# Mixer of a hybrid streaming encoder: readers of freshly loaded decay rows issued behind the eviction of the product traced last

## The chip, the cores and the metric

The kernel runs on one core of one Trainium2 chip. The metric is the device time of one execution in microseconds; the kernel before took 1926.99 us, the median of three runs (1923.51 to 1927.07).

## The reference

One layer of an encoder is computed for 512 prompt frames and 64 sample frames, 576 columns together, with 1024 channels: a SwiGLU block, a mixer, a second SwiGLU block, and a last RMSNorm. The mixer is one wide input projection that feeds three branches, whose outputs are projected, gated, added and projected once more. Two of the branches contain exponentials of cumulated decays, and they are what the change touches. Cut to that:

```python
# branch A, 16 heads in 4 groups, per chunk
cum  = jnp.cumsum(dtc * a, axis=1)
lmat = jnp.exp(jnp.where(causal, cum[:, :, None] - cum[:, None, :], -jnp.inf))
y = einsum((C B^T) * lmat * dt, x) + jnp.exp(cum) * einsum(C, h)
wd = jnp.exp(last[:, None] - cum) * dtc
h = jnp.exp(last) * h + einsum(wd, B, x)
# branch C, 4 heads, per chunk
s = einsum(q, k) * jnp.exp(logd - mt)
num = einsum(s, v) + jnp.exp(inter - mt) * einsum(q, c)
c = decay * c + einsum(jnp.exp(wlog - mnew), k, v)
```

Branch B is a banded softmax attention. All of it is in float32.

## The kernel before, in words

**Products.** Each weight product is made of three matmuls per block of 128 channels, since a float32 weight is split into a high and a low part (`split`, L333 to 335: ScalarE casts `ph`, VectorE subtracts for `pl`). In the mixer, weights come in pairs of columns and a pair takes seven products by Strassen's scheme (`pairs`, L608, over `stream`, L575). One product is 12 matmuls on TensorE (L704) into a PSUM bank `acc`. The pairs have three banks in turn, so a bank has to be evicted within a product or two, or TensorE stands still. Evictions are ScalarE copies (`uv` at L621, direct ones at L628 into `g`, `P` or `R`) and VectorE sums (L630). GpSimd adds weight blocks (L560) and issues accumulating loads of them (L548); SyncE issues the other loads.

**Jobs.** The branches are generators (`attn`, `ml` for branch C, `ssd` for branch A). They are traced a step at a time between the products (`tick`), so that their small matmuls fill in between. The order of the units is `a0 a1 m0 s0 a2 a3 s1 m1 s2 m2 s3 m3`; a unit `s` has two halves, each of two heads.

**Decay rows.** `gates` writes the cumulated decays of all heads to DRAM (`scr_rows`). `decays` (L188, on ScalarE's queue) loads two rows, spread over 128 partitions, into two slots of `R1`, named `R` in the profile; three such pairs of slots go round, and a load is issued one half unit ahead of its use. A half unit of `ssd` reads the rows with VectorE (`wd`, L1333 and L1334; the difference to all columns, L1349) and ScalarE (`el`, L1336 and L1337); then `wd` is exponentiated (L1338), the difference goes through Relu and Exp (L1352, L1358), is multiplied by `cb` on VectorE (L1360) and feeds the matmuls L1393. A second copy of the rows is loaded into the single buffer `ec` (L1356, two DMAs on ScalarE's queue), exponentiated (L1384) and used at L1403. A unit of `ml` reads its rows into the tile `D`, named `P` (L1162 on VectorE), exponentiates it (L1164, L1165), multiplies it by the causal mask on GpSimd (L1167, L1168) and by the scores on VectorE (L1173, L1176); `wc` (L1180) reads the rows on ScalarE.

**What sets the order.** Every engine carries out its instructions in the order in which they stand in its own queue. That order is made when the kernel is built, by a scheduler that plays the program through on a timeline of its own and takes what it holds ready, the tracing order deciding among equals; `high_priority(offset=EVAC)` puts evictions ahead. An edge (`issue_after`) makes the instructions traced within it stand behind a given instruction on that instruction's engine.

Of the kernel before, what the change touches and what calls it, by code (L numbers as in the profile page):

```python
# [28 lines left out]
AF = mybir.ActivationFunctionType  # L29
ALU = mybir.AluOpType  # L30
# [5 lines left out]
CH = [(0, 128), (128, 128), (256, 128), (384, 128), (512, 64)]  # L36
# [49 lines left out]
class Hybrid:  # L86
    def __init__(self, ctx, tc, I, O):
        self.tc, self.nc, self.I, self.O = tc, tc.nc, I, O
        self.op = None
        self.stay = {}  # L90
        self.plan = []
        self.splan = []
        self.ahead = {}
        self.steps = None
        self.b_i, self.b_n, self.fetched = 0, 0, deque()
        self.behind = 0
        self.jobs, self.gap, self.side = deque(), 0, iter(())
        nc = self.nc
        self.const = ctx.enter_context(tc.tile_pool(name="const", bufs=1))
        self.dram = ctx.enter_context(tc.tile_pool(name="scr", bufs=1, space=bass.MemoryType.DRAM))  # L100
        c = self.const
        self.R1 = c.tile([128, 8, T], F32, name="R1")
        self.rs = c.tile([128, T], F32, name="rs")
        self.small = ctx.enter_context(tc.tile_pool(name="small", bufs=8, reuse_waits="tile"))

        self.wt = ctx.enter_context(tc.tile_pool(name="wt", bufs=1, reuse_waits="tile"))
        self.xs = self.dram.tile([128, 8, T], F32, name="xs")

        self.ys = [self.dram.tile([128, T], F32, name=f"ys{i}") for i in range(16)]
        self.gs = [self.dram.tile([128, T], F32, name=f"gs{i}") for i in range(24)]  # L110
        self.scr = self.dram.tile([24, T], F32, name="scr_rows")
# [496 lines left out]
    def pairs(self, seq):  # L608

        nc = self.nc
        order = ((0, self.T_X1), (0, self.T_A11), (1, self.T_A22), (0, self.T_X4), (0, self.T_X3), (1, self.T_X2),
                 (0, self.T_A21))
        H = (slice(0, FH), slice(FH, T))

        def tmp(ps, scale):
            o = self.gp.tile([128, FH], F32, name="uv", tag="uv", bufs=4)
            with self.tc.high_priority(offset=EVAC):  # L620
                nc.scalar.activation(o, ps, AF.Copy, scale=scale)  # L621
            return o

        def emit(ps, scale, other=None, op=None):
            def go(dst, a=0, b=FH, func=None):
                with self.tc.high_priority(offset=EVAC):
                    if other is None:
                        nc.scalar.activation(dst, ps[:, a:b], func or AF.Copy, scale=scale)  # L628
                        return
                    nc.vector.scalar_tensor_tensor(dst, ps[:, a:b], scale, other[:, a:b], op0=ALU.mult, op1=op)  # L630
                if func:
                    nc.scalar.activation(dst, dst, func)
            return go

        def pair(tiles, done):
            ((name, c1), s1, put1), ((_, c2), s2, put2) = tiles
            o = {}

            def on(t, ps):
                if t == self.T_X1:  # L640
                    o["v"] = tmp(ps, s1)
                elif t == self.T_X4:
                    o["m6"] = tmp(ps, s2)
                elif t == self.T_A11:
                    put1(1, H[1], emit(ps, s1, o["v"], ALU.add))
                elif t == self.T_X3:
                    o["u"] = tmp(ps, s2)
                elif t == self.T_A21:
                    put2(1, H[1], emit(ps, s2, o["u"], ALU.subtract))
                elif t == self.T_A22:  # L650
                    put2(0, H[0], emit(ps, -s2, o["m6"], ALU.add))
                else:
                    put1(0, H[0], emit(ps, s1))
                    if done:
                        done()
            return (name, 0, c1, c2), self.T, on

        self.stream([pair(*p) for p in seq], order, lambda n: {self.T_X1: n % 2, self.T_X4: 2, self.T_A11: 2})

    def tick(self):
        next(self.side, None)
# [479 lines left out]
    def ml(self, h, t):  # L1144
        nc = self.nc
        q, k, v, o = t["q"], t["k"], t["v"], t["o"]
        i = self.b()
        nmB, eiB = self.R1[:, i, :], self.R1[:, i + 1, :]
# [6 lines left out]
        self.tok_major(v, v1)  # L1155
        yield 1
        qt = self.t("t")
        nc.gpsimd.tensor_tensor(qt, q, eiB, op=ALU.mult)

        D = self.P()  # L1160
        for c, (a, n) in enumerate(CH):
            nc.vector.tensor_scalar(D[:n, a:a + n], nmB[:n, a:a + n], self.TM[:n, c, 64 + h:65 + h], 0.0,  # L1162
                                    op0=ALU.add, op1=ALU.min)
        nc.scalar.activation(D[:, :512], D[:, :512], AF.Exp)  # L1164
        nc.scalar.activation(D[:64, 512:], D[:64, 512:], AF.Exp)  # L1165
        dv = D[:, :512].rearrange("p (c t) -> p c t", t=128)
# [2 lines left out]
        s = self.ps("s")  # L1169
# [6 lines left out]
        self.empties(nc.vector.tensor_tensor(D[:64, 512:], s2[:64, :64], D[:64, 512:], op=ALU.mult))  # L1176

        wc = self.unit([128, 8], "wc", 2)
        for c, (a, n) in enumerate(CH):
            nc.scalar.activation(wc[:n, c:c + 1], self.TM[:n, c, 64 + h:65 + h], AF.Exp, bias=nmB[:n, a + n - 1:a + n])  # L1180
        yield 2
        nums = [self.ps("v"), self.ps("x")]
        where = [(0, 0), (0, 129), (0, 258), (1, 0), (1, 129)]
# [1 line left out]
        for c, (a, n) in enumerate(CH):  # L1185
# [7 lines left out]
            if c == 0:  # L1193
                i = nc.vector.tensor_copy(C2[:, :129], pc[:, :129])
# [4 lines left out]
            b, o0 = where[c]  # L1199
# [12 lines left out]
        for c, (a, n) in enumerate(CH):  # L1212
            b, o0 = where[c]
# [68 lines left out]
    def ssd(self, g, t):  # L1282
# [26 lines left out]
        for j in range(2):  # L1309
# [18 lines left out]
            wd = self.unit([128, 5, 2], "wd", 2)  # L1328
            el = self.unit([128, 5, 2], "el", 2)
            nc.gpsimd.memset(wd[:, 4, :], 0.0)  # L1330
            for r in range(2):
                last = cum[r][:, 127:512:128]
                nc.vector.tensor_tensor(wd[:, 0:4, r], last, self.TM[:, 0:4, 32 + d0 + r], op=ALU.subtract)  # L1333
                nc.vector.tensor_tensor(wd[:64, 4:5, r], cum[r][:64, 575:576], self.TM[:64, 4:5, 32 + d0 + r],  # L1334
                                        op=ALU.subtract)
                nc.scalar.activation(el[:, 0:4, r], last, AF.Exp)  # L1336
                nc.scalar.activation(el[:, 4:5, r], cum[r][:, 575:576], AF.Exp)  # L1337
            nc.scalar.activation(wd, wd, AF.Exp)  # L1338
            for n, cs in ((128, slice(0, 4)), (64, slice(4, 5))):
                m = cs.stop - cs.start  # L1340
                nc.vector.tensor_tensor(h4(xw[:n, cs, :]), h4(xd[:n, cs, :]),
# [3 lines left out]
            for n, cs, ts in ((128, slice(0, 4), slice(0, 512)), (64, slice(4, 5), slice(512, T))):  # L1345
                m, w = cs.stop - cs.start, ts.stop - ts.start
                e = E[:n, :, ts].rearrange("p r (c t) -> p r c t", c=m)
                tm = self.TM[:n, cs, 32 + d0:34 + d0].rearrange("p c r -> p r c")
                nc.vector.tensor_tensor(e, e, tm.unsqueeze(3).broadcast_to([n, 2, m, w // m]), op=ALU.subtract)  # L1349
                parts.append(E[:n, :, ts])  # L1350
            for e in parts:
                nc.scalar.activation(e, e, AF.Relu, scale=-1.0)  # L1352
# [11 lines left out]
            for c, (a, n) in enumerate(CH):  # L1364
# [16 lines left out]
                    nc.sync.dma_start(self.O["s"][c - 3, :, d0 * 64:d0 * 64 + 128], new)  # L1381
                if c % 2:
                    yield 1
            nc.scalar.activation(ec, ec, AF.Exp)  # L1384
            D = self.cst[:, C_D + 2 * g + j:C_D + 2 * g + j + 1]
            py, pi = self.ps("v"), self.ps("x")
            for c, (a, n) in enumerate(CH):
# [364 lines left out]
```

## Time and profile before

| what | value |
|---|---|
| median of three runs | 1926.99 us (1923.51 to 1927.07) |
| the profiled execution | 1925.69 us, span 1924.0 us |
| TensorE busy in the span | 1865.2 us (97%) |
| VectorE, ScalarE, GpSimd busy | 1532.9, 1058.1, 654.1 us |
| first SwiGLU block, mixer, second SwiGLU block | about 0 to 570, 570 to 1355, 1355 to 1924 us |
| the stretch with pairs and jobs | 625 to 1195 us, TensorE busy 532.9 of 570.0 us |

A row of a timeline gives the start from the beginning of the span, the duration, the engine, the line, the operation and its tiles; idle time of the engine just before it stands in brackets with what ended it. The letter q after an engine marks its queue, that is, an issue of a DMA. In the view of waits a row gives who waited, for whom, the total in microseconds, how often, and the longest.

### The profile page before, as it was taken

Reading aid. Unit: us, or ns where it says so; the run is one execution under the profiler, and the core shown is the slowest. Engines: PE = TensorE matmul, PEld = TensorE weight load, DVE = VectorE, ACT = ScalarE, POOL = GpSimd, SP = SyncE. Lnnn points to the kernel's source line nnn. Section 1 sums busy time; section 2 is a strip of 40 time slices with the busy share of each in tenths; the row PEclk is TensorE's granted clock in tenths of the full one; section 3 lists DMA queues with packets and bytes.
Section 4 is the critical chain, followed back from the end, with each engine's and each line's share of the span. In section 5 each row is a group of like instructions: output and inputs, shape, how many; then the busy total and the mean of one; then the engine's idle time right before and its main releaser. Section 6 shows DMA issues by size and latency. Waiting matters only on the chain. (4 is left out here: it accounts for less than half of the span.)

```text
span 1924.0 us, 37528 instructions
## 1 busy us (share of the span) xinstructions
PE 1865.2 (97%) x13901; PEld 1815.5 (94%) x13901; DVE 1532.9 (80%) x2763; ACT 1058.1 (55%) x2342; POOL 654.1 (34%) x613
## 2 busy tenths in 40 slices
PE   9899999999999989999989989999999999999998
PEld 9899999999999879888989889999999999999998
DVE  7998998998768868678687766745898888898865
ACT  6554554554544776676665556324565455554544
POOL 3443333333302324323334333440334343333311
PEclk9999999999999999999999999999999999999999
DMA  7467666666742546755656655642546666666631
GB/s 222 104 158 177 154 164 159 156 176 164 184 135 89 146 130 161 214 147 144 176 141 183 171 143 173 208 175 82 128 111 159 170 159 166 164 156 169 153 99 56
DMA packets 129439, 294.69 MB, mean 153 GB/s; under 512 B 14288, under 2 KB 26192, under 8 KB 129256
## 3 DMA queue, kind: packets, MB, share of 16 engines
q1 hardware_dynamic: 99368, 203.42, 32.9%
q0 software_dynamic: 20272, 74.20, 21.1%
q10 hardware_dynamic: 9616, 14.69, 2.5%
q8 instruction: 109, 1.79, 0.4%
q14 instruction: 74, 0.61, 0.1%
HBM read 272.87 MB, written 19.38 MB: 152 GB/s over the span
## 5 line engine op out<-in xcount | busy, mean ns | idle before, releaser
L704 PE MATMUL acc<-TH,ph 128*128 128x288 f32 x3220 | 970.3, 302 | 34.2 <-ACT uv L621 16.4
L704 PE MATMUL acc<-TL,ph 128*128 128x288 f32 x3220 | 956.2, 297 | 0.8 <-DVE TL L335 0.7
L704 PE MATMUL acc<-TH,pl 128*128 128x288 f32 x3220 | 953.3, 296 | 0.3 <-DVE pl L335 0.3
L704 PEld LDWEIGHTS acc<-TH,ph 128*128 128x128 f32 x3220 | 607.8, 189 | 53.7 <-ACT uv L621 18.6
L704 PEld LDWEIGHTS acc<-TH,pl 128*128 128x128 f32 x3220 | 609.9, 190 | 2.9 <-issue 2.1
L704 PEld LDWEIGHTS acc<-TL,ph 128*128 128x128 f32 x3220 | 609.1, 189 | 3.0 <-DVE TL L335 2.0
L335 DVE TENSOR_TENSOR pl<-wr,ph 128x512 fp32r<-128x512 f32 x471 | 430.3, 919 | 70.3 <-ACT ph L334 59.0
L334 ACT CAST ph<-wr 128x512 fp32r<-128x512 f32 x471 | 287.2, 618 | 263.8 <-PE acc L704 142.5
L334 ACT CAST ph<-wx 128x512 fp32r<-128x512 f32 x390 | 237.1, 619 | 213.5 <-POOL wx L560 101.4
L335 DVE TENSOR_TENSOR pl<-wx,ph 128x512 fp32r<-128x512 f32 x390 | 312.3, 804 | 46.3 <-ACT ph L334 39.8
L560 POOL TENSOR_TENSOR wx<-wx,wr 128x512 f32<-128x512 f32 x160 | 246.5, 1540 | 178.9 <-DVE pl L335 143.6
L548 POOL DMA_DIRECT2D wx<-in_sblk x115 | 101.6, 917 | 522.3 <-DVE pl L335 204.4
L279 PE MATMUL acc<-YH,ph 128*128 128x256 f32 (+1 forms) x768 | 227.1, 298 | 3.0 <-ACT g L628 2.2
L279 PE MATMUL acc<-YL,ph 128*128 128x256 f32 (+1 forms) x768 | 227.1, 297 | 0.6 <-DVE YL L392 0.6
L279 PE MATMUL acc<-YH,pl 128*128 128x256 f32 (+1 forms) x768 | 226.7, 296 | 0.0
L279 PEld LDWEIGHTS acc<-YH,ph 128*128 128x128 f32 x768 | 145.0, 189 | 4.1 <-ACT g L628 2.3
L279 PEld LDWEIGHTS acc<-YL,ph 128*128 128x128 f32 x768 | 145.3, 189 | 1.1 <-DVE YL L392 1.0
L279 PEld LDWEIGHTS acc<-YH,pl 128*128 128x128 f32 x768 | 145.2, 189 | 0.0
L560 POOL TENSOR_TENSOR wy<-wx,wr 128x512 f32<-128x512 f32 x35 | 49.9, 1425 | 134.0 <-DVE pl L335 112.6
L743 DVE SCALAR_TENSOR_TENSOR R<-acc,R 128x288 f32<-128x288 f32 x168 | 75.7, 451 | 20.1 <-PE acc L704 19.8
L334 ACT CAST TH<-g 128x288 fp32r<-128x288 f32 x120 | 51.4, 433 | 50.4 <-POOL g L729 32.9
L335 DVE TENSOR_TENSOR pl<-wy,ph 128x512 fp32r<-128x512 f32 x70 | 54.4, 777 | 26.9 <-ACT ph L334 16.7
(329 smaller groups left out, 2328.7 us busy)
## 6 DMA issues: line engine op xcount, KB each, us to landing
wr<-in_sblk SPq DMA_DIRECT2D x345, 256.0 KB, 3.7
wx<-in_sblk POOLq DMA_DIRECT2D x119, 512.0 KB, 6.8
wx<-in_sblk SPq DMA_DIRECT2D x111, 512.0 KB, 3.8
wr<-in_wblk SPq DMA_DIRECT2D x126, 256.0 KB, 3.0
R<-scr_rows ACTq DMA_DIRECT2D x12, 576.0 KB, 5.8
gs<-g SPq DMA_DIRECT2D x20, 288.0 KB, 3.8
g<-gs POOLq DMA_DIRECT2D x20, 288.0 KB, 4.2
y<-ys POOLq DMA_DIRECT2D x12, 288.0 KB, 5.1
```

The lines of the kernel that those rows point to most:

```text
L279: last = nc.tensor.matmul(ps[:, :n], wt[:, wsl], xx[:, k0 + k, a:a + n], start=(k == 0 and i == 0), stop=(k == nk - 1 and i == 2))
L334: self.cast = self.nc.scalar.copy(hi, src).ins
L335: self.nc.vector.tensor_tensor(lo, src, hi.bitcast(F32), op=ALU.subtract)
L548: nc.gpsimd.dma_start(x12, src[:, 1:3, :], accum_op=ALU.add)
L560: add = lambda o, one, two: self.nc.gpsimd.tensor_tensor(o, one, two, op=ALU.add)
L704: self.nc.tensor.matmul(ps, wt[:, wsl], xx[:, kk, :], start=(start and kk == 0 and i == 0), stop=(kk == 3 and i == 2), skip_group_check=True)
L743: self.nc.vector.scalar_tensor_tensor(o, ps, scale, o, op0=ALU.mult, op1=ALU.add)
```

## The change

The kernel keeps the last traced eviction of a product on ScalarE and the last one on VectorE (`evicted`). A new context, `behind_products`, gives every instruction traced inside an edge to the one of these two that is on its own engine. The readers of the decay rows are put inside it: `D` (L1162) and `wc` (L1180) in `ml`; `wd`, `el`, the exponential of `wd`, the difference at L1349, and the exponential of `ec` (L1384) in `ssd`. One GpSimd product (`qt`, L1158) is kept in program order. No instruction is added or taken away, 11 activation tables are loaded in both programs, and from the last products of the mixer on the order is the same.

```diff
+        self.evicted = {}
...
-                nc.scalar.activation(o, ps, AF.Copy, scale=scale)
+                self.evicted["ACT"] = nc.scalar.activation(o, ps, AF.Copy, scale=scale).ins
...
-                        nc.scalar.activation(dst, ps[:, a:b], func or AF.Copy, scale=scale)
+                        self.evicted["ACT"] = nc.scalar.activation(dst, ps[:, a:b], func or AF.Copy, scale=scale).ins
                         return
-                    nc.vector.scalar_tensor_tensor(dst, ps[:, a:b], scale, other[:, a:b], op0=ALU.mult, op1=op)
+                    self.evicted["DVE"] = nc.vector.scalar_tensor_tensor(dst, ps[:, a:b], scale, other[:, a:b],
+                                                                         op0=ALU.mult, op1=op).ins
...
+    @contextmanager
+    def behind_products(self):
+        with ExitStack() as s:
+            for i in self.evicted.values():
+                s.enter_context(self.tc.issue_after(i))
+            yield
...
-        nc.gpsimd.tensor_tensor(qt, q, eiB, op=ALU.mult)
+        self.tc.keep_in_program_order(nc.gpsimd.tensor_tensor(qt, q, eiB, op=ALU.mult))
         D = self.P()
-        for c, (a, n) in enumerate(CH):
-            nc.vector.tensor_scalar(D[:n, a:a + n], nmB[:n, a:a + n], self.TM[:n, c, 64 + h:65 + h], 0.0,
+        with self.behind_products():
+            for c, (a, n) in enumerate(CH):
+                nc.vector.tensor_scalar(D[:n, a:a + n], nmB[:n, a:a + n], self.TM[:n, c, 64 + h:65 + h], 0.0,
...
+        with self.behind_products():
+            for c, (a, n) in enumerate(CH):
+                nc.scalar.activation(wc[:n, c:c + 1], self.TM[:n, c, 64 + h:65 + h], AF.Exp, bias=nmB[:n, a + n - 1:a + n])
...
+            with self.behind_products():
+                for r in range(2):
+                    last = cum[r][:, 127:512:128]
+                    nc.vector.tensor_tensor(wd[:, 0:4, r], last, self.TM[:, 0:4, 32 + d0 + r], op=ALU.subtract)
...
+                    nc.scalar.activation(el[:, 0:4, r], last, AF.Exp)
+                    nc.scalar.activation(el[:, 4:5, r], cum[r][:, 575:576], AF.Exp)
+                nc.scalar.activation(wd, wd, AF.Exp)
...
+                with self.behind_products():
+                    nc.vector.tensor_tensor(e, e, tm.unsqueeze(3).broadcast_to([n, 2, m, w // m]), op=ALU.subtract)
...
-            nc.scalar.activation(ec, ec, AF.Exp)
+            with self.behind_products():
+                nc.scalar.activation(ec, ec, AF.Exp)
```

The lines of the changed kernel are up to 15 higher: L1356 is L1370, L1384 is L1399, L1180 is L1192, L621 is L622, L1167 is L1178.

**ScalarE, second half of unit s3.** `ec<-scr_rows` are the two loads of `ec`, `ec<-ec` its exponential; `uv<-acc` and `g<-acc` are evictions of products. Before:

```order
L1356 DMA ec<-scr_rows 64x576
L334 CAST ph<-wx 128x512
L1356 DMA ec<-scr_rows 64x576
...
L1371 COPY st<-ps_s 128x128
L1384 ACT_TABLE_LOAD
L1384 ACTIVATE ec<-ec 128x576
L334 CAST ph<-wy 128x512
L621 ACTIVATE uv<-acc 128x288 x2
L334 CAST ph<-wy 128x512
L628 ACTIVATE g<-acc 128x288
```

and with the change:

```order
L1370 DMA ec<-scr_rows 64x576
L1366 ACTIVATE R_60<-R_60 128x2x512
L1366 ACTIVATE R_60<-R_60 64x2x64
L335 CAST ph<-wr 128x512
L1370 DMA ec<-scr_rows 64x576
...
L629 ACTIVATE g<-acc 128x288
...
L622 ACTIVATE uv<-acc 128x288 x2
L335 CAST ph<-wx 128x512
L622 ACTIVATE uv<-acc 128x288
L1399 ACTIVATE ec<-ec 128x576
```

The exponential stood ahead of three evictions and now stands behind those three and a fourth. The Relu of this half's differences (L1352, now L1366) has come in between: before, it ran 83 us ahead of the load's issue (at 1050.71 us, the load at 1133.72 us).

**ScalarE, unit m2.** The reader `wc` of the rows before, between the load's issue and an eviction:

```order
L334 CAST ph<-wr 128x512
L1220 ACTIVATE junk,ss<-ps_x,r 64x128
L1180 ACTIVATE wc<-TM,R_60 128x1 x4
L1180 ACTIVATE wc<-TM,R_60 64x1
L334 CAST ph<-wr 128x512
L1263 COPY co<-P 128x3
L1264 COPY co<-P 128x3
L334 CAST ph<-wy 128x512
L628 ACTIVATE P<-acc 128x288
```

and with the change the reader of the same kind in the unit m2, which now stands some 40 products later:

```order
L629 ACTIVATE g<-acc 128x288
L335 CAST ph<-wy 128x512
L622 ACTIVATE uv<-acc 128x288 x2
L1009 COPY t<-ps_x 128x4x128
L335 CAST ph<-wx 128x512
L622 ACTIVATE uv<-acc 128x288
L1192 ACTIVATE wc<-TM,R_60 128x1 x4
L1192 ACTIVATE wc<-TM,R_60 64x1
```

**GpSimd, mask product of unit m1.** `P<-P,mask` is the mask product, `wx<-in_sblk` the accumulating load. Before, the mask product of m1 ran at 880.34 us, 72 us ahead of the first matmul that uses it (L1201, 952.51 us). With the change:

```order
L561 TENSOR_TENSOR wy<-wx,wr 128x512
L561 TENSOR_TENSOR wy<-wy,wr 128x512
L549 DMA wx<-in_sblk 128x1024
L1178 TENSOR_TENSOR P<-P,mask 128x512
L1179 TENSOR_TENSOR P<-P,mask 64x64
L561 TENSOR_TENSOR wy<-wx,wr 128x512
```

The mask product of this unit now stands behind the issue of an accumulating load, and the VectorE products that use it follow at once.

More of the change, by code (lines that the diff above doesn't have):

```diff
@@ L1157, in ml @@
         qt = self.t("t")
-        nc.gpsimd.tensor_tensor(qt, q, eiB, op=ALU.mult)
+        self.tc.keep_in_program_order(nc.gpsimd.tensor_tensor(qt, q, eiB, op=ALU.mult))
         D = self.P()
-        for c, (a, n) in enumerate(CH):
-            nc.vector.tensor_scalar(D[:n, a:a + n], nmB[:n, a:a + n], self.TM[:n, c, 64 + h:65 + h], 0.0,
-                                    op0=ALU.add, op1=ALU.min)
+        with self.behind_products():
+            for c, (a, n) in enumerate(CH):
+                nc.vector.tensor_scalar(D[:n, a:a + n], nmB[:n, a:a + n], self.TM[:n, c, 64 + h:65 + h], 0.0,
+                                        op0=ALU.add, op1=ALU.min)
         nc.scalar.activation(D[:, :512], D[:, :512], AF.Exp)
@@ L1178, in ml @@
         wc = self.unit([128, 8], "wc", 2)
-        for c, (a, n) in enumerate(CH):
-            nc.scalar.activation(wc[:n, c:c + 1], self.TM[:n, c, 64 + h:65 + h], AF.Exp, bias=nmB[:n, a + n - 1:a + n])
+        with self.behind_products():
+            for c, (a, n) in enumerate(CH):
+                nc.scalar.activation(wc[:n, c:c + 1], self.TM[:n, c, 64 + h:65 + h], AF.Exp, bias=nmB[:n, a + n - 1:a + n])
         yield 2
@@ L1330, in ssd @@
             nc.gpsimd.memset(wd[:, 4, :], 0.0)
[L1331 to L1338, printed above, removed]
+            with self.behind_products():
+                for r in range(2):
+                    last = cum[r][:, 127:512:128]
+                    nc.vector.tensor_tensor(wd[:, 0:4, r], last, self.TM[:, 0:4, 32 + d0 + r], op=ALU.subtract)
+                    nc.vector.tensor_tensor(wd[:64, 4:5, r], cum[r][:64, 575:576], self.TM[:64, 4:5, 32 + d0 + r],
+                                            op=ALU.subtract)
+                    nc.scalar.activation(el[:, 0:4, r], last, AF.Exp)
+                    nc.scalar.activation(el[:, 4:5, r], cum[r][:, 575:576], AF.Exp)
+                nc.scalar.activation(wd, wd, AF.Exp)
             for n, cs in ((128, slice(0, 4)), (64, slice(4, 5))):
@@ L1348, in ssd @@
                 tm = self.TM[:n, cs, 32 + d0:34 + d0].rearrange("p c r -> p r c")
-                nc.vector.tensor_tensor(e, e, tm.unsqueeze(3).broadcast_to([n, 2, m, w // m]), op=ALU.subtract)
+                with self.behind_products():
+                    nc.vector.tensor_tensor(e, e, tm.unsqueeze(3).broadcast_to([n, 2, m, w // m]), op=ALU.subtract)
                 parts.append(E[:n, :, ts])
```

## The prediction

> **What bounds the kernel now.** I read the page first, then the windows by stage, then the waits of TensorE and ScalarE in the mixer's stretch of pairs and jobs, and last the timelines around the waits.
>
> ```profile
> span 1924.0 us, 37528 instructions
> PE 1865.2 (97%) x13901; PEld 1815.5 (94%) x13901; DVE 1532.9 (80%) x2763; ACT 1058.1 (55%) x2342; POOL 654.1 (34%) x613
> ...
> 625.00:1195.00 570.00, 532.90 (x4003) 494.17 (x4001) 422.02 (x924) 374.07 (x949) 199.47 (x196) 0.98 0.59 160
> ```
>
> TensorE bounds it: it idles for 58.8 us of 1924.0, and 37.1 of these (570.00 less 532.90) lie in this stretch. The change moves only instructions here, so 37.1 us is all that it can win. Who ends this idle time, and what ScalarE waits for in the same stretch:
>
> ```profile
> PE acc L704 <- ACT uv L621: 16.4, 12, 3.6
> PE acc L704 <- ACT P L628: 5.7, 3, 3.3
> ...
> ACT ec L1384 <- DMA ec<-scr_rows: 10.2, 5, 3.3
> ACT wc L1180 <- DMA R<-scr_rows: 7.2, 4, 3.5
> ```
>
> TensorE waits above all for late evictions on ScalarE, and ScalarE for rows that have not landed. That the one makes the other is seen at the places themselves: each pair is ScalarE's wait and TensorE's idle time just behind it.
>
> ```profile
> 781.11 0.68 ACT L1384 ACTIVATE ec<-ec 128x576 f32<-128x576 f32 x1 [1.31 <-DMA ec<-scr_rows]
> 782.14 0.43 PE L704 MATMUL acc<-TH,ph 128*128 128x288 f32 x1 [1.39 <-ACT uv L621]
> ...
> 926.13 0.68 ACT L1384 ACTIVATE ec<-ec 128x576 f32<-128x576 f32 x1 [3.25 <-DMA ec<-scr_rows]
> 927.78 0.40 PE L704 MATMUL acc<-TH,ph 128*128 128x288 f32 x1 [2.98 <-ACT uv L621]
> ...
> 969.51 1.03 ACT L1180 ACTIVATE wc<-TM,R 128x1 f32<-128x1 f32 x5 [1.75 <-DMA R<-scr_rows]
> 972.12 0.40 PE L704 MATMUL acc<-TH,ph 128*128 128x288 f32 x1 [1.51 <-ACT P L628]
> ...
> 1033.52 0.68 ACT L1384 ACTIVATE ec<-ec 128x576 f32<-128x576 f32 x1 [1.84 <-DMA ec<-scr_rows]
> 1035.17 0.61 PE L704 MATMUL acc<-TH,ph 128*128 128x288 f32 x1 [1.81 <-ACT uv L621]
> ...
> 1078.51 1.03 ACT L1180 ACTIVATE wc<-TM,R 128x1 f32<-128x1 f32 x5 [3.50 <-DMA R<-scr_rows]
> 1081.12 0.40 PE L704 MATMUL acc<-TH,ph 128*128 128x288 f32 x1 [3.25 <-ACT P L628]
> ...
> 1134.32 0.64 ACTq L1356 DMA_DIRECT2D ec<-scr_rows  x1
> 1141.63 1.28 ACT L1384 ACT_TABLE_LOAD   x1 [3.92 <-DMA ec<-scr_rows]
> 1144.48 0.61 PE L704 MATMUL acc<-TH,ph 128*128 128x288 f32 x1 [3.56 <-ACT uv L621]
> ```
>
> Six idle times, nearly as long as the waits: a reader stands too soon behind its load, and the evictions queue behind it.
>
> **Term A, the six waits.** In the changed order each `wc` stands some 40 products behind its load, so its rows are there. The exponential of `ec` stands behind the four evictions that it held up. That removes 1.39 + 2.98 + 1.51 + 1.81 + 3.25 + 3.56 = 14.5 us. A rest may stay in s1, s2 and s3: the second load lands 7.3 us after its issue (1134.32 to 1141.63), and between the two the new order has one Relu, two Exp, a square, casts and evictions, together about 5.8 us by the durations here. Up to 1.5 us of wait is then left, but the next eviction comes five products later. A product takes 2.3 us with its share of job work: 570 us over 244, a quarter of the matmuls in this row.
>
> ```profile
> L704 PE MATMUL acc<-TH,ph 128*128 128x288 f32 x976 | 304.0, 312 | 25.2 <-ACT uv L621 16.4 <-ACT P L628 5.7 <-DVE R L630 1.7
> ec<-scr_rows ACTq DMA_DIRECT2D x16, 144.0 KB, 5.9
> ```
>
> The casts queued behind it are made several products ahead. So A is -14.5, at worst -10. The Trainium skill, in "DMA: Bandwidth & Descriptors", section "Anatomy of one DMA", gives a DMA about 2.0 us plus its bytes at 436 GB/s; an estimate by that page for 144 KB is 2.3 us, and then no row would be late and A would be nothing. The row says 5.9 us in the median and the timeline 7.3; I go by these.
>
> **Term B, the start of the stretch.** Before, the readers of both halves of s0 ran at 670 to 685 us, amid the softmax of the second attention unit; now they stand 30 to 40 products later.
>
> ```profile
> 678.96 1.25 ACT L1358 ACTIVATE R<-R 128x1024 f32<-128x1024 f32 x2
> ...
> 683.30 1.24 ACT L1358 ACTIVATE R<-R 128x1024 f32<-128x1024 f32 x2
> ...
> 681.97 0.76 PE L1044 MATMUL ps_x<-ident,P 128*128 128x128 f32 x5 [1.10 <-ACT P L1035]
> 684.21 0.66 PE L997 MATMUL ps_x<-ident,g 128*128 128x128 f32 x4 [1.48 <-DVE Q L1048]
> 685.40 0.40 PE L704 MATMUL acc<-TH,ph 128*128 128x288 f32 x1 [0.54 <-ACT g L628]
> ```
>
> Three idle times of TensorE, 3.1 us together, follow these exponentials. The softmax chain keeps some of them; between 0 and -3.1 I take -2.0.
>
> **Term C, the half units' chain.** Nothing is added, but what ran up to 80 us ahead now runs just before its use, between evictions. Per half unit that is the difference, Relu, Exp and the product with `cb`:
>
> ```profile
> L1360 DVE TENSOR_TENSOR R<-R,t 128x1024 f32<-128x1024 f32 x8 | 12.7, 1627 | 0.0
> ...
> L1349 DVE TENSOR_TENSOR R<-R,TM 128x1024 f32<-128x1024 f32 x8 | 9.8, 1220 | 0.6 <-ACT el L1336 0.6
> ...
> L1352 ACT ACTIVATE R<-R 128x1024 f32<-128x1024 f32 x8 | 8.5, 1059 | 2.0 <-DVE R L1349 2.0
> L1358 ACT ACTIVATE R<-R 128x1024 f32<-128x1024 f32 x8 | 8.4, 1052 | 0.0
> ```
>
> 1.63 + 1.22 + 1.06 + 1.05 = 5.0 us. Does ScalarE have room? In the stretch of s1's first half, between two evictions:
>
> ```profile
> 897.84 0.62 ACT L334 CAST ph<-wr 128x512 fp32r<-128x512 f32 x1 [0.23 <-PE acc L704]
> 899.86 0.62 ACT L334 CAST ph<-wx 128x512 fp32r<-128x512 f32 x1 [1.41 <-PE acc L704]
> 901.21 0.45 ACT L632 ACTIVATE g<-g 128x288 f32<-128x288 f32 x1 [0.73 <-DVE g L630]
> ...
> 902.78 0.45 ACT L632 ACTIVATE g<-g 128x288 f32<-128x288 f32 x1 [0.54 <-DVE g L630]
> ...
> 906.07 0.62 ACT L334 CAST ph<-wy 128x512 fp32r<-128x512 f32 x1 [2.27 <-PE acc L704]
> ```
>
> It idles 0.23 + 1.41 + 0.73 + 0.54 + 2.27 = 5.2 us. What comes in is a table load (1.28), the small exponentials (about 0.7), Relu and Exp of both parts (1.25 each): 4.5 us. It fits with 0.7 us to spare, if no wait stands in the wrong place; Relu has to wait for VectorE's difference, so some will. TensorE's place for L1393 has moved one to six products later, which covers part of it. Bounds: 0, and 4.5 less one product's 2.3, so 2.2 us for each of the eight half units. I take 0.5, near the end that the room speaks for: +4.0.
>
> **Term D, the mask products.** In m1, m2 and m3 the chain through GpSimd was hidden tens of microseconds ahead. Now it stands behind an accumulating load in m1 and m2:
>
> ```profile
> 950.64 0.33 SPq L544 DMA_DIRECT2D wx<-in_sblk  x1
> 952.51 0.61 PE L1201 MATMUL ps_v<-t,P 128*128 128x129 f32 x4
> 955.09 0.87 POOL L548 DMA_DIRECT2D wx<-in_sblk  x1 [6.07 <-DVE cs L1196]
> ...
> L1167 POOL TENSOR_TENSOR P<-P,mask 128x512 f32<-128x512 f32 x4 | 13.2, 3296 | 5.4 <-ACT P L1164 5.4
> ```
>
> The accumulating load waits 4.5 us for the plain load of its buffer (950.64 to 955.09). At that time the mask product would end at 955.09 + 0.87 + 3.30 = 959.3, while L1201, now two products later, is due at 952.51 + 4.6 = 957.1: 2.2 us late. But the split that frees that buffer also stands some products earlier in the new order, by up to 4 us. So 0 to 2.2 us for each of the three units; I take 0.5: +1.5. The Trainium skill, in "SBUF — State Buffer", under "Practical consequences", says that VectorE with two SBUF inputs shuts out a GpSimd instruction that reads SBUF for its whole length, and the other way round. The mask product's 3.30 us agrees; if it kept clear of VectorE, as an addition of 1.29 us does, D would be 0.
>
> **The sum.** -14.5 - 2.0 + 4.0 + 1.5 = -11.0. The profiled execution took 1925.69 us (1.69 around its span stay), so 1914.7; the median of the runs is 1.3 above that execution, so **1916**. With A's -10 to -14.5, B's 0 to -3.1, C up to 8 and D up to 4.5 the forecast's own range is about 1909 to 1926.
>
> **The rivals.**
> 1. The wait only moves: the exponential of `ec` still stands too soon for a load of 7.3 us, and holds up evictions in s1 to s3 by the 1.5 us above; 3 x 1.5 = 4.5 back, 1920. For it: the loads are issued as late as before. Against: the four evictions are already done. Chance 0.13, still faster.
> 2. The chain eats the gain: C at 1.3 us for each half and D at 0.7 give +12.5; -16.5 + 12.5 = -4, 1923, within 0.2% (3.9 us, what a measurement here can tell from no change). For it: 0.7 us to spare is little. Chance 0.14.
> 3. Slower: TensorE stands at L1393 and L1201 in every unit, since difference, Relu, Exp and `cb` product cross between VectorE and ScalarE in their queues behind evictions. At 3 us for each of 8 halves and 2.2 for three units it is 30.6 against 16.5: +14, 1941. It decides from 1.5 us of lateness at each of the 11 places. Against: their places on TensorE moved back with the chain. Chance 0.09.
> 4. The rows are not the cause (the page's 2.3 us): nothing changes, 1927. The six pairs speak against it. Chance 0.02.
>
> **How the numbers follow.** The forecast has 0.62. Faster: 0.62 + 0.13 = 0.75; same 0.14 + 0.02 = 0.16; slower 0.09. The range 1907 to 1927 takes in the forecast's bounds and rivals 1, 2 and 4; only the slower case and a gain beyond A and B are left out.
>
> **What would show it.** Right: no row of ScalarE's waits with `scr_rows` at `wc`, and at `ec` only ones that no eviction follows; TensorE's wait for `uv` from 16.4 to under 6 us, and its busy time in the stretch unchanged. C shows as TensorE waiting for L1360's result at L1393, or for an eviction just behind Relu and Exp; D as TensorE waiting at L1201 or VectorE at L1173 for GpSimd's mask. I am wrong if the stretch is not shorter by about 11 us, or if these new waits come to over 12.

## The result and the profile after

The changed kernel takes 1916.88 us (median of 19 runs, 1911.97 to 1921.37), the kernel before beside it 1924.04 us (19 runs, 1916.74 to 1929.90). The ratio is 0.9963, with a 95% interval of 0.9952 to 0.9974: 7.1 us faster (5.0 to 9.2). The forecast was 11 us faster, and 1916 us.

The page of the changed kernel; its profiled execution took 1918.76 us:

```profile
span 1917.1 us, 37553 instructions
PE 1863.0 (97%) x13901; PEld 1814.7 (95%) x13901; DVE 1535.8 (80%) x2763; ACT 1061.2 (55%) x2342; POOL 661.5 (35%) x613
```

To compare the mixer's stretch, I cut it in both traces at the same two products, and read the windows (the columns: window, its length, then busy time and instructions of TensorE, its weight loads, VectorE, ScalarE and GpSimd, then the granted clock of TensorE, the DMA share and GB/s). Before:

```profile
622.53:1200.34 577.81, 539.77 (x4043) 500.68 (x4044) 428.43 (x934) 377.33 (x954) 204.25 (x201) 0.98 0.59 160
```

and after:

```profile
6.83:625.60 618.77, 609.17 (x4512) 603.64 (x4510) 530.14 (x882) 327.64 (x673) 204.83 (x174) 0.99 0.58 156
625.60:1194.25 568.65, 536.17 (x4042) 497.32 (x4043) 436.96 (x934) 378.98 (x954) 211.93 (x202) 0.98 0.58 163
```

The stretch is 9.2 us shorter. Only 5.6 us of that is idle time of TensorE (577.81 - 539.77 = 38.0 before, 568.65 - 536.17 = 32.5 after). The other 3.6 us are busy time: the same matmuls take less. The block ahead of it, which the change doesn't touch, took 618.8 us here and 616.1 before; over all the profiles of this study it lies between 615.4 and 618.8, so that is scatter.

The waits in the changed kernel between 625 and 1195 us (who waited for whom: total, times, longest):

```profile
PE acc L714 <- ACT g L629: 8.4, 3, 3.9
PE acc L714 <- ACT uv L622: 6.6, 8, 1.1
...
PE ps_s L1382 <- DVE t L1354: 2.3, 3, 1.2
...
PE ps_v L1408 <- DVE R L1374: 1.6, 1, 1.6
...
ACT R L1366 <- POOL wd L1342: 7.8, 2, 3.9
...
ACT ec L1399 <- DMA ec<-scr_rows: 1.0, 1, 1.0
```

The late rows are gone: ScalarE waits 1.0 us for the rows of `ec` in place of 10.2 and the 3.9 ahead of the table load, not at all at `wc`, and TensorE's wait for `uv` fell from 16.4 to 6.6 us. None of the six idle times behind late rows is left. But two new ones of 3.9 us each stand behind the eviction `g` (L629), in the second halves of s1 and s2: counted in TensorE's order, ahead of the same two products that waited 2.98 and 1.81 us before. 3.9 us more stand behind the half units' own products (L1354 and L1374). Here is the first of the two, in the changed kernel's timeline:

```profile
915.00 0.41 ACT L346 ACTIVATE sq<-R 128x256 f32<-128x256 f32 x1
918.77 0.46 ACTq L1370 DMA_DIRECT2D ec<-scr_rows  x1
919.33 1.06 ACT L1366 ACTIVATE R<-R 128x1024 f32<-128x1024 f32 x1 [3.92 <-POOL wd L1342]
...
921.37 1.24 ACT L1372 ACTIVATE R<-R 128x1024 f32<-128x1024 f32 x2
922.52 0.60 ACT L335 CAST ph<-wy 128x512 fp32r<-128x512 f32 x1
923.03 0.40 ACT L629 ACTIVATE g<-acc 128x288 f32<-128x288 f32 x1
...
923.48 0.40 PE L714 MATMUL acc<-TH,ph 128*128 128x288 f32 x1 [3.92 <-ACT g L629]
```

ScalarE stands for 3.92 us ahead of Relu (L1366), and the eviction stands behind Relu and Exp. The row names GpSimd's memset of `wd` as what ended the wait. But the issue of the load of `ec` (L1370, marked q) stands between, and it was carried out at 918.77 us. At that time GpSimd and VectorE show:

```profile
915.06 1.41 DVE L1363 TENSOR_TENSOR R<-R,TM 128x1024 f32<-128x1024 f32 x2
...
915.21 3.52 POOL L1420 TENSOR_TENSOR g<-g,ec 128x64 f32<-128x64 f32 x1 [0.98 <-DVE g L1411]
...
916.40 0.88 DVE L1354 TENSOR_TENSOR t<-t,wd 128x512 f32<-128x512 f32 x2
...
918.17 0.41 DVE L347 TENSOR_TENSOR sumsq<-sumsq,sq 128x256 f32<-128x256 f32 x1
```

The addition L1420 is the last reader of the old contents of `ec`. It ended at 915.21 + 3.52 = 918.73 us, 0.04 us ahead of the load's issue. It is 64 columns wide and takes 0.3 to 1.2 us at its six other places in the mixer; here, and at 1021.81 us, it takes 3.52 us, beside a VectorE that works without a pause from 915.06 to 918.58 us, with the difference L1363 that the change put there.

### The profile page after: what moved, and what is told of

The parts are those of the page before. It is cut to its first block, busy times and chain, and to the rows that moved or that the text cites. A ratio compares the mean times of both kernels' runs of the same rounds, so it can differ in the third digit from the quotient of the medians.

```text
span 1917.1 us, 37553 instructions
## 1 busy us (share of the span) xinstructions
PE 1863.0 (97%) x13901; PEld 1814.7 (95%) x13901; DVE 1535.8 (80%) x2763; ACT 1061.2 (55%) x2342; POOL 661.5 (35%) x613
## 5 line engine op out<-in xcount | busy, mean ns | idle before, releaser
L714 PE MATMUL acc<-TH,ph 128*128 128x288 f32 x3220 | 965.8, 301 | 28.8 <-ACT g L629 8.4
L561 POOL TENSOR_TENSOR wy<-wx,wr 128x512 f32<-128x512 f32 x35 | 59.7, 1706 | 141.1 <-DVE pl L336 109.7
L739 POOL TENSOR_TENSOR g<-g,P 128x288 f32<-128x288 f32 x56 | 62.3, 1112 | 35.7 <-ACT P L738 35.7
```

The source lines that it names most:

```text
L561: add = lambda o, one, two: self.nc.gpsimd.tensor_tensor(o, one, two, op=ALU.add)
L714: self.nc.tensor.matmul(ps, wt[:, wsl], xx[:, kk, :], start=(start and kk == 0 and i == 0), stop=(kk == 3 and i == 2), skip_group_check=True)
L739: nc.gpsimd.tensor_tensor(s["g"][:, 1, :], s["g"][:, 1, :], a, op=ALU.mult)
```

## The experiments

All of them, with the stretch cut at the same two products (before: 577.8 us, of which TensorE is idle 38.0):

| edit | median, us | ratio to before (95% interval) | stretch, us | TensorE idle in it, us |
|---|---|---|---|---|
| the change | 1916.9 | 0.9963 (0.9952 to 0.9974) | 568.7 | 32.5 |
| 1: a second tile for `ec` | 1913.5 | 0.9938 (0.9920 to 0.9957) | 568.3 | 31.6 |
| 2: memset of `wd` on VectorE | 1913.6 | 0.9937 (0.9920 to 0.9955) | 570.2 | 32.0 |
| 3: no edge at `ec` | 1918.6 | 0.9969 (0.9953 to 0.9985) | 570.6 | 34.2 |
| 4: no edges at `wd`, `el`, differences | 1902.3 | 0.9876 (0.9859 to 0.9893) | 554.1 | 24.4 |
| 5: load of `ec` from GpSimd | 1910.4 | 0.9939 (0.9923 to 0.9954) | 563.6 | 29.8 |
| 6: no edge at `wd`, `el` | 1911.9 | 0.9946 (0.9929 to 0.9962) | 561.9 | 27.7 |
| 7: edge at `ec` alone | 1924.6 | 1.0008 (0.9996 to 1.0019) | 572.5 | 33.8 |
| 8: `wd`, `el`, differences late in s0 alone | 1902.5 | 0.9905 (0.9887 to 0.9923) | 552.4 | 19.8 |
| 9: addition L1420 on VectorE | 1904.4 | 0.9896 (0.9875 to 0.9916) | 558.2 | 21.9 |
| 10: edges at `D` and `wc` alone | 1919.6 | 0.9973 (0.9959 to 0.9988) | 570.7 | 34.0 |
| 11: as 8, load of `ec` from GpSimd | 1906.2 | 0.9901 (0.9882 to 0.9921) | 556.6 | 28.8 |
| 12: as 8, addition L1420 on VectorE | 1907.4 | 0.9917 (0.9899 to 0.9934) | 557.4 | 26.6 |

### What the two new waits of 3.9 us are

**Run 1, a second tile for `ec`.**

```diff
-            ec = self.unit([128, T], "ec", 1)
+            ec = self.rs if j else self.unit([128, T], "ec", 1)
```

> The changed kernel, but the second copy of the rows in the second half of each unit s goes to another tile (rs, which lies idle in this stretch), so two of them go round in place of one. Theory 1 (the load of ec waits in ScalarE's queue until GpSimd's addition L1420 has read the old contents, and Relu, Exp and the eviction stand behind it): the two idle times of TensorE of 3.92 and 3.94 us in s1 and s2 fall under 0.5 us each, about 1909 us against 1916.9 of the changed kernel. Theory 2 (Relu itself waits for GpSimd's memset of wd, as the row names it): both stay, 1917. Theory 3 (it is the work of Relu and Exp ahead of the eviction, 4.3 us, not the wait): at least 2 us stay at each place, 1913 to 1917.

Both idle times stayed, at 3.93 us. That seems to speak against theory 1, but the timeline shows that the edit did not take the wait away:

```profile
911.71 3.52 POOL L1420 TENSOR_TENSOR g<-g,ec 128x64 f32<-128x64 f32 x1 [0.98 <-DVE g L1411]
...
915.27 0.46 ACTq L1370 DMA_DIRECT2D ec<-scr_rows  x1
915.83 1.06 ACT L1366 ACTIVATE R<-R 128x1024 f32<-128x1024 f32 x1 [3.93 <-POOL wd L1342]
```

With two tiles the order puts each load one half unit earlier. The load that stands ahead of this Relu is that of the next unit, into the tile that L1420 still reads: it goes out at 915.27 us, 0.04 us after the addition (911.71 + 3.52). The run does not decide.

**Run 2, the memset on VectorE.**

```diff
-            nc.gpsimd.memset(wd[:, 4, :], 0.0)
+            nc.vector.memset(wd[:, 4, :], 0.0)
```

> The changed kernel with the memset of wd on VectorE in place of GpSimd; the order on ScalarE around the two places is the same. Theory 1 (single buffer of ec): the idle times of 3.92 and 3.94 us stay, 1917 us. Theory 2 (the memset on GpSimd is what Relu waits for): both go, about 1909. Theory 3: both stay, 1917.

The order on ScalarE is the same, and both waits stayed (3.92 and 3.94 us at TensorE):

```profile
917.20 1.06 ACT L1366 ACTIVATE R<-R 128x1024 f32<-128x1024 f32 x1 [3.92 <-POOL R L1423]
```

The memset is gone from GpSimd, and the row now names the next instruction there, L1423. So the name was no cause, only what ended last on that engine. Theory 2 falls. The medians of runs 1 and 2 lie 3 us below the changed kernel's, though the stretch is as long; I have no cause for that and read nothing from it.

**Run 5, the load of `ec` from GpSimd's queue.**

```diff
-                nc.scalar.dma_start(ec[r * 64:(r + 1) * 64, :], self.rows(d0 + r, 64))
+                nc.gpsimd.dma_start(ec[r * 64:(r + 1) * 64, :], self.rows(d0 + r, 64))
```

> The changed kernel with the two loads of ec issued from GpSimd's queue, behind its addition L1420, in place of ScalarE's. Relu, both Exp and the eviction keep their order on ScalarE; only the load and what it waits for leave that queue. Theory 1 (ScalarE stands at the load until L1420 has read the old contents): the idle times of 3.92 and 3.94 us of TensorE in s1 and s2 fall under 1 us each; 7 to 9 us off, ratio to before about 0.992, near 1910 us. Theory 3 (the work of Relu and Exp ahead of the eviction): at least 2 us stay at each place, 1914 us or above.

TensorE's two idle times fell from 3.92 and 3.94 to 2.80 and 2.08 us: less than theory 1 says. By the bounds set beforehand the time is theory 1's (near 1910 us), the idle times are theory 3's (at least 2 us left at each place). What is left:

```profile
909.30 3.52 POOL L1420 TENSOR_TENSOR g<-g,ec 128x64 f32<-128x64 f32 x1 [0.98 <-DVE g L1411]
...
910.45 1.06 ACT L1366 ACTIVATE R<-R 128x1024 f32<-128x1024 f32 x1 [0.95 <-DVE R L1363]
913.23 0.47 ACT L346 ACTIVATE sq<-R 128x320 f32<-128x320 f32 x1 [1.72 <-POOL R L1423]
...
916.43 0.61 PE L714 MATMUL acc<-TH,ph 128*128 128x288 f32 x1 [2.80 <-ACT g L629]
```

ScalarE no longer stands at the load. It stands 0.95 us for the late difference, and then 1.72 us at the square L346, which reads the product L1423 that GpSimd makes just behind the same slow addition. So theory 1 named one of two instructions that wait for GpSimd. Without the square's wait 1.1 us of the 2.80 would be left, and at the second place, where the square waits 0.81 us, 1.3 us of the 2.08: by this estimate Relu, Exp and the wait for the difference, theory 3's share, are worth about 1 us at each place. Theory 4 came from this: the common cause is the addition. (It took 3.52 us at the first place in this run, and 0.90 us at the second.)

**Run 9, the addition L1420 on VectorE.**

```diff
-            nc.gpsimd.tensor_tensor(x[:, 515:], x[:, 515:], ec[:, 512:], op=ALU.add)
+            nc.vector.tensor_tensor(x[:, 515:], x[:, 515:], ec[:, 512:], op=ALU.add)
```

> The changed kernel with the addition L1420 (128x64) on VectorE in place of GpSimd. Theory 4 (the common cause of both places is this addition: 3.52 us at 915 and 1022 us where it stands beside the late difference L1363 on VectorE, against 0.60 elsewhere; the load of ec and the square L346 on ScalarE both wait for GpSimd behind it): the idle times of 3.92 and 3.94 us fall under 1 us each, stretch from 898 to 1179 us shorter by 6 us or more, ratio to before about 0.992. Theory 3 (Relu, Exp and casts ahead of the eviction are too much work by themselves): at least 2 us stay at each place, ratio 0.995 or above.

Both idle times went, and the time with them, from 1916.9 to 1904.4 us. TensorE's waits for `g` in the mixer, 8.4 us in the changed kernel:

```profile
PE acc L714 <- ACT g L629: 1.0, 2, 0.6
```

and the window of the stretch:

```profile
624.64:1182.80 558.16, 536.30 (x4043) 496.17 (x4043) 441.21 (x942) 378.92 (x954) 211.05 (x194) 0.98 0.60 166
```

Between the products at 898.63 and 1179.49 us of the changed kernel it is 268.2 us in place of 280.9. Moving one addition of 64 columns, eight times in the program, with the order that the scheduler then made, thus gave back more than the whole change had won. But GpSimd was not rid of its slow instruction:

```profile
918.38 0.21 DVE L1420 TENSOR_TENSOR g<-g,ec 128x64 f32<-128x64 f32 x1
...
918.66 3.93 POOL L1423 TENSOR_TENSOR R<-g,R 128x64 f32<-128x64 f32 x1
...
920.16 0.38 ACT L629 ACTIVATE g<-acc 128x288 f32<-128x288 f32 x1
...
922.62 0.47 ACT L346 ACTIVATE sq<-R 128x320 f32<-128x320 f32 x1 [1.20 <-POOL R L1423]
```

The addition takes 0.21 us on VectorE, and GpSimd's next product, L1423, takes 3.93 us in place of 0.30. The square still waits 1.20 us for it, but it now stands behind the eviction `g`, and the load of `ec` stands behind Relu, not ahead of it. So the edit changed the order too: it shows that the idle times go when nothing that waits for GpSimd stands ahead of the eviction, and that Relu and an Exp ahead of it cost next to nothing, so theory 3 falls for these two. It does not show that this one addition is the cause, nor does it tell apart the square's share and the load's.

### Which of the edges give and which take

**Run 4, the rows of the units s early.** The edges at `wd`, `el`, the exponential of `wd` and the differences are taken away; those at `D`, `wc` and `ec` stay.

```diff
-            with self.behind_products():
+            if True:
                 for r in range(2):
...
-                with self.behind_products():
+                if True:
                     nc.vector.tensor_tensor(e, e, tm.unsqueeze(3).broadcast_to([n, 2, m, w // m]), op=ALU.subtract)
```

> The changed kernel without the edges at wd, el and the differences of the units s: these run early again as before; D and wc of the units m and the exponential of ec stay behind the products. If the half units' chain just ahead of its use is what gives part of the gain back (term C: 4.0 us predicted, and the waits seen at L1382, L1408 and behind the load of ec come to about 11 us in the trace), the time falls to 1907 to 1913 us, with TensorE's 1.4 to 3.1 us at the start of s0 (term B) back. Rival (the chain costs nothing and the differences must be late): 1917 or above.

1902.3 us: below the range expected, and the fastest kernel of the study, by 1.24% of the kernel before.

The addition in its timeline:

```profile
910.59 0.60 POOL L1420 TENSOR_TENSOR g<-g,ec 128x64 f32<-128x64 f32 x1
```

and the window of the stretch:

```profile
623.65:1177.73 554.08, 529.70 (x4043) 492.57 (x4043) 431.74 (x934) 379.21 (x954) 193.21 (x199) 0.99 0.61 166
```

With the differences early again, the addition takes 0.60 us, no idle time of 3.9 us is left, and Relu and Exp stand behind the eviction again. The stretch is 14.6 us shorter than in the changed kernel: 8.1 us less idle, and 6.5 us less busy time for the same 4043 matmuls.

**Run 6, `wd` and `el` early, the differences late.**

```diff
-            with self.behind_products():
+            if True:
                 for r in range(2):
```

> The changed kernel without the edge at wd and el; the differences of the units s stay behind the products. In this order the loads of ec stand behind Exp in place of ahead of Relu. If the late differences (VectorE) with Relu and Exp (ScalarE) are what gives the gain back, most of the 14 us between the changed kernel and the one with all of it early stay lost: 1911 to 1917 us. If wd and el just ahead of their use are (TensorE at L1382, and VectorE's wd of 1.3 us each), about 1903 to 1907.

1911.9 us: of the 14.6 us of the stretch, 6.7 came back (568.7 to 561.9). The other 7.8 us are the late differences' with Relu and Exp. It is no clean halving, since here too the order has put the load of `ec` behind Exp, and L1420 takes 1.28 us.

**Run 3, no edge at `ec`.**

```diff
-            with self.behind_products():
-                nc.scalar.activation(ec, ec, AF.Exp)
+            nc.scalar.activation(ec, ec, AF.Exp)
```

> The changed kernel without the edge at the exponential of ec; all the other readers stay behind the products. By term A of the prediction: that exponential is now held off by the half's Relu, Exp and casts (5.8 us against a load of up to 7.3 us), so up to 1.5 us of wait at each of s1, s2 and s3 comes back: 1917 to 1921 us, TensorE's waits behind it 0 to 4.5 us together. Rival (the edge at ec carries the gain, and the moved rows matter little): its four waits come back at their old 9.7 us, 1926.

1918.6 us, as term A's rest says and not the rival's 1926, but the interval holds the changed kernel too. ScalarE waits 13.2 us for the rows of `ec` again, but TensorE's longest wait for `uv` is 1.4 us (3.6 in the kernel before). With the half units' chain late, this edge is worth 2 us or nothing.

**Runs 7 and 10, one part alone.** Run 7 has the edge at `ec` and no other; run 10 has those at `D` and `wc` (and the product `qt` in program order) and no other. Against the changed kernel, run 7, cut to the lines on `qt`, `D`, `wc`, `wd` with `el`, and the difference:

```diff
-        self.tc.keep_in_program_order(nc.gpsimd.tensor_tensor(qt, q, eiB, op=ALU.mult))
+        nc.gpsimd.tensor_tensor(qt, q, eiB, op=ALU.mult)
...
-        with self.behind_products():
-            for c, (a, n) in enumerate(CH):
...
+        for c, (a, n) in enumerate(CH):
...
-        with self.behind_products():
+        if True:
...
-            with self.behind_products():
+            if True:
...
-                with self.behind_products():
+                if True:
```

and run 10, cut to the lines on `wd` with `el`, the difference, and `ec`:

```diff
-            with self.behind_products():
+            if True:
...
-                with self.behind_products():
+                if True:
...
-            with self.behind_products():
-                nc.scalar.activation(ec, ec, AF.Exp)
+            nc.scalar.activation(ec, ec, AF.Exp)
```

> The kernel before with one of the edges: the exponential of ec stands behind the products, all other readers as before. By the idle times alone (1.39 + 2.98 + 1.81 + 3.56 = 9.7 us) the ratio is 0.995, some 1916 us. If each of these waits also costs the slow stretch seen behind it (pitch of the matmuls 240 ns in place of 133 for 11 to 15 of them, 1.2 to 1.6 us each, 5.5 us together), it is 0.992, some 1910 us.

> The kernel before with the edges at D and wc of the units m alone (and the product qt in program order). By term A the two waits at wc go: 1.51 + 3.25 = 4.8 us, 1920 us or a ratio of 0.9975. If the edge at ec gives nothing (as alone) and these give the whole gain of the kernel with ec, D and wc (ratio 0.9876), it is 0.988 to 0.990. If the two only work together, it is 0.996 to 1.000.

Run 10 gave 0.9973, 5.2 us, about the 4.8 us of its two waits. That the two numbers meet is luck. ScalarE waits for no row at `wc` any more, but ahead of the same two products (972.12 and 1081.12 us before) TensorE still idles, now behind other evictions:

```profile
972.65 0.40 PE L714 MATMUL acc<-TH,ph 128*128 128x288 f32 x1 [1.47 <-ACT uv L622]
...
1077.25 0.40 PE L714 MATMUL acc<-TH,ph 128*128 128x288 f32 x1 [1.28 <-ACT uv L622]
```

That is 2.75 us in place of 4.76; ahead of the four products that waited behind `ec` it is 5.1 us in place of 9.7, with no edge there.

Run 7 gave nothing in time, though ahead of its four products no idle time is left. In its trace the stretch is 5.3 us shorter, but the rest of the span is 3.4 us longer. Its waits show one reason why the stretch did not win more, its timeline another (L1369, L1191 and L1419 are the changed kernel's L1370, L1192 and L1420):

```profile
ACT wc L1191 <- DMA R<-scr_rows: 5.4, 2, 2.9
```

```profile
1047.75 0.45 ACTq L1369 DMA_DIRECT2D ec<-scr_rows  x1
1048.24 0.59 ACT L1009 COPY t<-ps_x 128x512 f32<-128x512 f32 x1 [3.50 <-POOL g L1419]
...
1048.88 0.55 PE L1007 MATMUL ps_x<-ident,g 128*128 128x128 f32 x3 [2.44 <-ACT t L1009]
```

The waits at `wc` are still there, and the next load of `ec` stands 3.50 us in ScalarE's queue for GpSimd, with a copy and two evictions behind it. Together (run 4) the two edges gave 23.9 us at 0.9876, against 5.2 and nothing alone. That they don't add up is measured. Part of the reason is the waits that each alone leaves to the other. Another part is TensorE's clock. In the traces the stretch is shorter than before by 23.7 us (run 4), 7.1 (run 10) and 5.3 (run 7), and of this 10.1, 3.1 and 1.1 us are busy time. The traces' records of the granted clock have it at a half for 27.3 us of the stretch before, and for 6.8, 20.5 and 23.9 us in these three runs; half of what is gone is 10.2, 3.4 and 1.7 us, which is about that busy time. Why the two edges together also save more idle time (13.7 us against 4.0 and 4.2) is shown only in part.

### Versions that go further

**Run 8: `wd`, `el` and the differences late in s0 alone.**

```diff
-            with self.behind_products():
+            with self.behind_products() if g == 0 else nullcontext():
...
-                with self.behind_products():
+                with self.behind_products() if g == 0 else nullcontext():
```

> The kernel with the edges at D, wc and ec, and those at wd, el and the differences in unit s0 alone. Term B (readers of s0 out of the softmax's way): 2 us below the kernel without the edges in s0 (1902), so 1900 us, with TensorE's idle times at L1007 and at the products behind it around 685 us gone. Rival (they are kept by the softmax chain itself): 1902, no difference.

In the trace the stretch is the shortest of all, 552.4 us, and its first part, to the product at 751.05 us of the kernel before, takes 121.7 us against 124.0 in run 4: term B, 2.3 us (3.4 us by TensorE's idle time). The medians of runs 8 and 4 are the same, so no gain is shown in time.

**Runs 11 and 12** are run 8 with the load of `ec` issued by GpSimd (the edit of run 5), and with the addition on VectorE (the edit of run 9).

```diff
-                nc.scalar.dma_start(ec[r * 64:(r + 1) * 64, :], self.rows(d0 + r, 64))
+                nc.gpsimd.dma_start(ec[r * 64:(r + 1) * 64, :], self.rows(d0 + r, 64))
```

```diff
-            nc.gpsimd.tensor_tensor(x[:, 515:], x[:, 515:], ec[:, 512:], op=ALU.add)
+            nc.vector.tensor_tensor(x[:, 515:], x[:, 515:], ec[:, 512:], op=ALU.add)
```

> The kernel with D, wc and ec behind the products everywhere and wd, el and the differences in s0 alone, and the two loads of ec issued from GpSimd's queue in place of ScalarE's. If the load of ec still holds up ScalarE there (COPY t at L1009 stands 3.72 us behind GpSimd's L1420 at 1032 us, TensorE 2.38 us behind it, and a slow stretch of 0.9 us), those 2 to 3 us go: ratio 0.989 against 0.9905. Rival (GpSimd's own queue is late by the two issues of about 0.6 us each, and its additions of weights with it): no change or slower.

> The kernel of the run with late readers in s0 only, with the addition L1420 on VectorE in place of GpSimd. There the load of ec and COPY t at L1009 still stood 3.72 us behind GpSimd's additions (1032 us), TensorE 2.38 us behind them with a slow stretch of 0.92 us. If GpSimd's additions ahead of the load are what makes it late, about 2 us go: ratio 0.9890 to 0.9895 against 0.9905. If the wait is mostly for the first addition L1419 (1.31 us, starting behind the accumulating load at 1028.65), it stays: 0.9905.

Neither is faster than run 8. In run 11 the wait went from the load to the square:

```profile
930.25 0.42 ACT L346 ACTIVATE sq<-R 128x256 f32<-128x256 f32 x1 [3.32 <-POOL R L1422]
...
931.38 0.30 PE L1011 MATMUL ps_x<-ident,g 128*64 128x128 f32 x1 [3.53 <-DVE t L1013]
```

ScalarE waits 3.32 us for GpSimd's product, VectorE behind it, and TensorE 3.53 us for a copy on VectorE. In run 12 ScalarE's copy L1009 still stands 3.50 us (3.72 in run 8). The load ahead of it goes out at 1034.91 us, 0.03 us behind the end of the other addition, L1419 (1033.57 + 1.31), so there it was that one that held it, as the expectation's second branch has it.

## Why the prediction was right, and where it was not

**The time** was right (1916 against 1916.9), the direction too, and the size of the gain within the forecast's own range (7.1 against 11; 9.2 in the stretch of the profiled execution). That the time agrees to 1 us is luck. The prediction started from 1926.99 us, the median of three runs, where 19 runs of the kernel before give 1924.04. And term C was 7.8 us too low, while the clock's 3.6 us, which no term held, and 1.5 us of D that did not come stood against it. The range was not added up rightly either: -10 + 8 + 4.5 is 2.5 us slower, 1929.5 and not 1926, and the 2.2 us bounded for each of eight half units would be 17.6, not 8.

**Term A, the six waits: right in the trace, wrong as a sum.** None of the six waits for rows is left, 14.5 us, as priced; at two of the six products another wait has taken the place, and it is counted under C. Two things were missed. First, a wait costs more than its idle time, so the 37.1 us of idle time were not all that the change could win. The windows of the kernel before just behind the waits (length, TensorE's busy time and instructions; the granted clock is the third number from the end):

```profile
782.14:785.74 3.60, 3.60 (x16) 3.60 (x17) 1.19 (x3) 1.68 (x4) 1.28 (x1) 0.53 0.12 37
...
929.20:932.50 3.30, 3.30 (x16) 3.30 (x15) 2.37 (x5) 2.78 (x6) 1.66 (x2) 0.50 0.07 20
...
1035.17:1038.20 3.03, 3.03 (x12) 3.03 (x13) 2.72 (x6) 3.03 (x6) 1.84 (x2) 0.50 0.00 0
1144.48:1147.50 3.02, 3.02 (x12) 3.02 (x13) 2.71 (x6) 1.54 (x4) 1.84 (x2) 0.50 0.10 36
1081.12:1084.50 3.38, 3.38 (x25) 3.38 (x26) 3.38 (x12) 3.31 (x9) 2.26 (x2) 1.00 0.27 83
```

At the full clock 25 matmuls take 3.38 us, 0.135 each. Behind four of the six waits the clock fell to a half for some 3 us; the 56 matmuls in these windows took 12.95 us in place of 7.6, which is 5.4 us on top of the idle time. This is where the busy time went that the stretch lost; a part came back behind both of the new waits, in the same view of the changed kernel:

```profile
925.00:928.00 3.00, 3.00 (x18) 2.67 (x19) 3.00 (x4) 1.91 (x4) 2.09 (x2) 0.50 0.00 0
...
1030.38:1033.79 3.41, 3.41 (x17) 3.41 (x16) 2.83 (x7) 1.82 (x6) 1.98 (x2) 0.50 0.08 29
```

Over the whole stretch the granted clock was a half for 27.3 us before and for 20.5 us with the change. Half of the difference is 3.4 us, against the 3.6 us that the busy time fell.

Second, the waits don't add up place by place: run 7 took four of them away and gained nothing in time.

**Term B, the start of s0: about right.** The idle time up to the product at 751.05 us fell by 1.8 us (11.0 to 9.2); runs 8 and 4 differ by 2.3 us. Predicted: 2.0.

**Term C, the half units' chain: this step failed.** Predicted 4.0, at most 8; the two waits of 3.9 us and those at L1382 and L1408 come to 11.8 us of idle time, and the kernel without this part of the change is 14.6 us faster. The step that failed is "It fits with 0.7 us to spare": I counted the room on ScalarE alone. ScalarE nearly had the room: run 5 leaves about 1 us at each of the two places to its work and its wait for the difference. What came in its way was GpSimd: the difference L1349 (now L1363), put just ahead of its use, keeps VectorE busy while GpSimd makes its addition, and the addition is what ScalarE's next load waits for, and its square just behind it. In run 9 another of GpSimd's instructions was as slow beside a busy VectorE, so by these rows it is the busy VectorE beside it that makes it slow, not the addition itself; no run isolates it. Nothing in the diff touches that addition. Its row stood in the trace of before with 0.6 us, and with the single buffer that ties ScalarE's queue to it.

**Term D, the mask products: 0 in place of +1.5.** No wait of TensorE at the matmuls of the mask's products (L1213, L1201 before) is left in the changed kernel's waits. In m1 the plain load went out at 943.99 us in place of 950.64, so the accumulating load did too (948.26 in place of 955.09). And the mask product itself, priced at 3.30 us, took 1.29 to 1.89 us in the four units.

**The sum in idle time**: -14.5 (A), -1.8 (B), +11.8 (C), about -1.1 in small places, is the -5.6 of the windows; the clock adds -3.6. Of the rivals, 2 (the chain eats the gain) had the right kind of loss and nearly its size (+12.5 for C and D against 11.8); without the clock's part it would about have come true (-4.5 and the small places, against its -4). Rival 1 happened in part: the wait of the exponential of `ec` did move, not to itself but to its load. Rival 4's 2.3 us for a load of `ec` was seen on neither queue: the median is 5.9 us before and 4.0 with the change, and 4.5 in run 5, where GpSimd issues it.

**The signs.** The waits for rows at `wc` are gone, and C showed as an eviction behind Relu and Exp, as named. Two signs did not come: TensorE's wait for `uv` fell to 6.6 us and not under 6, and its busy time in the stretch did not stay but fell by 3.6 us. The new waits, 11.8 us, stayed just under the 12 that would have made the prediction wrong by its own words.

## What to carry to other kernels

An instruction that is moved is not only to be priced on its own engine's room: ask which instructions of the other engines it will now stand beside, and who waits for those. A DMA that reloads a single buffer is a wait in the queue that issues it, as long as the last reader of the buffer is late; in the profile it hides behind the name of whatever ended last on that reader's engine, so look for the queue's own rows between. And edges that each cure one wait are to be tried apart and together: here one alone gave nothing, one took back most of what the others won, and leaving that one out more than tripled the gain.

## What was not expected of the hardware

- **Short waits can halve TensorE's clock.** Idle times of 1.39 and 1.81 us were followed by about 3 us at a granted clock of 0.50 to 0.53, one of 3.25 us (at 1081.12 us) by none. The Trainium skill, in "TensorE: Matmul & The Clock Gate", section "Part 1: The HAM clock gate", says that the clock is halved after an idle window of about 3.4 us, and that the window runs freely. The half clock agrees with the rows, and so does the free-running window: in the stretch before, the seven spans at half the clock last 3.41 us (one 6.83) and start whole multiples of 3.41 us apart. That the window has to be idle does not agree. The windows ahead of the span at 782.37 us, and around the wait of 3.25 us:

```profile
778.96:782.37 3.41, 1.62 (x9) 1.27 (x10) 2.33 (x8) 2.10 (x8) 1.26 (x1) 1.00 0.99 360
...
1075.92:1079.33 3.41, 1.94 (x15) 1.71 (x13) 0.96 (x3) 0.82 (x5) 1.68 (x1) 1.00 0.88 204
1079.33:1082.75 3.42, 1.63 (x12) 1.64 (x13) 2.67 (x9) 3.42 (x11) 0.51 (x1) 1.00 0.36 105
```

In the 3.41 us ahead of the seven spans TensorE was busy for 0.14 to 1.74 us, so a window idle for about half its length could be enough. The wait of 3.25 us lay across two windows, busy for 1.94 and 1.63 us, and the clock stayed full. So where a wait falls among the windows counts; a sharp border is not shown, since 1.63 us busy left the clock full here and 1.74 us elsewhere did not.
- **An addition of 128x64 on GpSimd took 3.52 us in place of 0.60** where VectorE worked through without a pause beside it (at 915 and at 1022 us in the changed kernel, and again in runs 1, 2, 3 and 5), and 0.60 where the differences were elsewhere (run 4). With the addition gone from GpSimd (run 9) its product L1423 took 3.93 us in place of 0.30. The Trainium skill, in "SBUF — State Buffer", section "Who interferes with whom", says that such an instruction of GpSimd is blocked until the one on VectorE is done. Here it ended only 0.15 us after a row of VectorE's instructions of 3.5 us together, not after the first of them (two in 1.41 us).
